# One decoder layer on one core: a 64-byte constant, small weights laid out by the host, and a tail by halves

## The chip, the cores and the metric

The kernel runs on one core of a Trainium2 chip. The metric is device microseconds per execution, the median of several runs. The profile shows one more execution, instruction by instruction.

## The reference

One layer of a hybrid decoder on 512 positions of width 1024, in float32:

```python
def reference(x, ...):
    h = rmsnorm(x, norm_mix_g)
    # h @ w_in, cut into conv gate/value, q, k, v, z of 8 gated-DeltaNet heads, a, b and two merge gates
    # a short gated convolution branch and a gated delta rule branch (chunks of 64), each with an output product
    # sigmoid-gated merge, product with w_o, residual add
    # rmsnorm, conv_ffn: (silu(conv(h @ w_up)[gate]) * conv(...)[value]) @ w_down, residual add
    # final rmsnorm with norm_final_g
...
def rmsnorm(x, g):
    xf = x.astype(jnp.float32)
    y = xf * lax.rsqrt(jnp.mean(xf * xf, axis=-1, keepdims=True) + EPS)
    return (y * g.astype(jnp.float32)).astype(x.dtype)
```

The large products are 1024 to 9216 (and 16 more columns, called ab below), 1024 to 1024 three times, 1024 to 2 x 2816 and 2816 to 1024. The three convolutions have 3 or 4 taps per channel; their weights, the norms' scales and two vectors of 8 numbers per head are the "small weights".

## The kernel before, in words

**Products.** Each float32 operand is split into a rounded part and a rest, which the code calls hi and lo: `wh` and `wl` for weights, `hT[0]` and `hT[1]` for the normalised input, and so on. A product is then three products: hi by lo, lo by hi, hi by hi. Weights come in blocks: one load of 1 MB fills a tile `raw`; `Block.split` makes four pairs wh, wl of it, ACT casting (line 140) and DVE subtracting (line 141), while the block before is used. Nearly all products go through the helper `mm` on line 108, so they differ in a profile by the tiles, where the streaming operand is named first and the stationary one second. In the helper, too, work of other engines is stepped along, after every so many columns. Several products are done in forms that need fewer multiplications: the first with sums of its input (`ts`; for w_up `us`), the product with w_o (`mix`, `mixb`), and the one with w_down (`xs`).

**Where tiles stand.** A tile has the same bytes in all 128 partitions, and each is rounded up to 32 bytes. Pools are stacked from two sides. On the left come the constants (`const`: gate, ident, nhalf, phalf, wA, wF), then the weights (raw, wh, wl), then hT, h, yb and others; on the right what one stage needs (`ts`, `yas`, `mix`, `mixb`, `us`, `xs`). The constants end at byte 2816 of a partition, a multiple of 256, and the sizes that follow are such that every left tile of the products begins at a multiple of 256. The right tiles named here begin at 224 in 256.

**The head** (lines 426 to 575). SP issues the loads in the order of the source. The rows of x are four tiles of 128 rows; the first two are done first: the sum of squares on ACT (`norm_x`), a root on POOL, scaling on DVE (`scale_x`), transposes on PE (`turn_x`), and from PSUM the two parts of hT, `out_hi` on ACT and `out_lo` on DVE. The block K of w_in is loaded in quarters (`load_k`), cast by `round_k` and subtracted by `rest_k`. PE does six products with a tile of zeros (`warm`; three in the program, each runs as two instructions) while it waits. DVE, ACT and POOL follow the source's order here (`manual_schedule`); PE's order is a scheduler's. The small weights arrive as rows (wr, wr2, wr3), are transposed on PE and copied by DVE into wA (scales and conv weights of the first stage) and wF (those of the feed-forward part); dtb and alg are loaded as broadcasts. A scheduler orders what comes behind this block, among it the casts of the next `raw`.

**The tail.** The product with w_down ends with blocks of `LAST` slots: `use_t` twice, then `use_l`. In `use_l` each of the row tiles 2 and 3 takes its last 12 products of 512 columns into one bank of PSUM (`v4`), and `fin2` follows: x-add on DVE, squares on ACT, product with the scale on DVE, the root on POOL, scaling by it of one half on DVE and of the other on ACT, two stores. (The other half of these rows is done earlier, by `fin2_hi`.)

Of the kernel before, what the change touches and what calls it, by code (L numbers as in the profile page):

```python
# [9 lines left out]
F32 = mybir.dt.float32  # L10
# [6 lines left out]
P = 128  # L17
# [42 lines left out]
@with_exitstack  # L60
def layer_kernel(ctx, tc, x, norm_mix_g, w_in, w_ab, conv_a_w, gdn_conv_w, gdn_A_log, gdn_dt_bias,
                 gdn_norm_g, w_a_out, w_b_out, w_o, norm_ffn_g, w_up, ffn_conv_w, w_down,
                 norm_final_g, out):
# [154 lines left out]

    gate = const.tile([1, 1], F32, name="gate")

    def feed(raw):
        el = raw[0:1, 1].rearrange("p k n -> p (k n)") if len(raw.shape) == 4 else raw[0:1, 1]
        tc.keep_in_program_order(pool.tensor_copy(out=gate, in_=el[:, 0:1]))  # L223
        advance(adds, FEED)
# [202 lines left out]
    with tc.tile_pool(name="st1", bufs=1) as st1:  # L427
# [19 lines left out]
        nc.sync.dma_start(out=wr[96:120], in_=conv_a_w.rearrange("o j (c p) -> (o j c) p", p=P))  # L447
        nc.sync.dma_start(out=wr[120:128], in_=norm_mix_g.rearrange("o (c p) -> (o c) p", p=P))
# [7 lines left out]
        load_k(2)  # L456
        dtb = gs.tile([P, H], F32, name="dtb")
        nc.sync.dma_start(out=dtb, in_=gdn_dt_bias[0].partition_broadcast(P))
        alg = gs.tile([P, H], F32, name="alg")
        nc.sync.dma_start(out=alg, in_=gdn_A_log[0].partition_broadcast(P))  # L460
        fr = ffn_conv_w.rearrange("o j (c p) -> (o j c) p", p=P)
        wr2 = st1.tile([66, P], F32, name="wr2")
        nc.sync.dma_start(out=wr2, in_=fr[0:66])
        wr3 = st1.tile([67, P], F32, name="wr3")
        nc.sync.dma_start(out=wr3[0:66], in_=fr[66:132])
        nc.sync.dma_start(out=wr3[66:67], in_=gdn_norm_g)

        po = bank()
        for _ in range(WARM):
            pe.matmul(po[:, 0:512], lhsT=warm[:, 0:P], rhs=warm[:, 0:512], start=True, stop=True)  # L470
        po = bank()
        sst = st1.tile([P, 2 * NT], F32, name="sst")
# [55 lines left out]
        with tc.manual_schedule(engines={mybir.EngineType.DVE, mybir.EngineType.Activation, mybir.EngineType.Pool}):  # L528
# [12 lines left out]
            o_ab, o_k = bank(), [bank(), bank()]  # L541
            for ks in (lower, upper):
                for k in ks:
                    out_hi(0, bs, k)
                for k in ks:
                    out_lo(0, bs, k)
                    k_tile(0, k)
                    ab_tile(k)
                if ks is lower:
                    rest_k(1)  # L550
# [21 lines left out]
        po = bank()  # L572
        pe.transpose(out=po[:, 0:66], in_=wr2, identity=ident[:66, :66])
        pe.transpose(out=po[:, 66:133], in_=wr3, identity=ident[:67, :67])
        dve.tensor_copy(out=wF, in_=po[:, 0:133])

# [655 lines left out]

    def times(o, xs, slot, i, tau, wh, wl, start=False, stop=False, free=False):
        xh, xl = (e[:, slot, i, tau * P:(tau + 1) * P] for e in xs)
        for k, (a, b) in enumerate(((xl, wh), (xh, wl), (xh, wh))):
            mm(o, a, b, start and k == 0, stop and k == 2, free)

# [4 lines left out]

    def times_b(banks, xs, slot, names, tau, wh, wl, q=None, start=False, stop=False):
        for name, i in names:
            o, w = banks["11" if name == "21" else name][tau], name if q is None else (name, q)
            times(o, xs, slot, i, tau, wh[w], wl[w], start and name != "21", stop, name == "21")

# [247 lines left out]
    def use_b(p):  # L1495
        def use(wh, wl):
            if p % 2 == 0 and p // 2 + 1 < N7 // 2:
                splits.append(prep_d(prep_b, p // 2 + 1))
            for name in (*FORMS_T, *FORMS_B):
                for tau in range(2):  # L1500
                    times_b(d_banks, xs(), p % 4, (name,), tau, wh, wl)
            if p == N7 - LAST - 1:
                splits.append(prep_d(prep_b, N7 // 2 - 1))
        return use


    def use_t(q):
        def use(wh, wl):
            for tau in range(2):
                for i in range(2):  # L1510
# [3 lines left out]
        return use  # L1514

    def use_l(wh, wl):
        for tau in range(2):
            for i in range(LAST):
                times_b(d_banks, xs(), (N7 - LAST + i) % 4, FORMS_B, tau, wh, wl, i, False, i == LAST - 1)
            fin2(tau + 2, [d_banks["v4"][tau]])  # L1520

# [14 lines left out]
    def fin2(t, acc):  # L1536
        cvp, x1 = st["cvp"], st["x1"]
        ss = cvp.tile([P, 2], F32, tag="ss", name=nm("ss"))
        if t < 2:
            o = pair_out()  # L1540
            y, r = [o[:, sl] for sl in HALVES], cvp.tile([P, 1], F32, tag="r", name=nm("r"))
        else:
            y, r = st["y", t], st["r", t]
        for hf, a in enumerate(acc):
            sl = HALVES[hf]
            dve.tensor_tensor(out=x1[:, t, sl], in0=x1[:, t, sl], in1=a, op=ALU.add)
            act.activation(out=a, in_=x1[:, t, sl], func=AF.Square, accum_out=ss[:, hf:hf + 1])
            dve.tensor_tensor(out=y[hf], in0=x1[:, t, sl], in1=st["gfn"][:, sl], op=ALU.mult)
            if hf < len(acc) - 1:
                dve.tensor_scalar(r, ss[:, hf:hf + 1], 1.0 / D, EPS, op0=ALU.mult, op1=ALU.add)  # L1550
        dve.scalar_tensor_tensor(out=r, in0=ss[:, len(acc) - 1:len(acc)], scalar=1.0 / D, in1=r,
                                 op0=ALU.mult, op1=ALU.add)
        pool.tensor_tensor(out=r, in0=r, in1=nhalf[:, 0:1], op=ALU.pow)
        dve.tensor_scalar(y[0], y[0], r, None, op0=ALU.mult)
        act.activation(out=y[1], in_=y[1], func=AF.Copy, scale=r)
        for sl, e in zip(HALVES, y):
            nc.sync.dma_start(out=out2[t * P:(t + 1) * P, sl], in_=e)


    def down_place(i):  # L1560
# [18 lines left out]

_INS = ['x', 'norm_mix_g', 'w_in', 'w_ab', 'conv_a_w', 'gdn_conv_w', 'gdn_A_log', 'gdn_dt_bias', 'gdn_norm_g',  # L1580
        'w_a_out', 'w_b_out', 'w_o', 'norm_ffn_g', 'w_up', 'ffn_conv_w', 'w_down', 'norm_final_g']
_OUTS = [((1, 512, 1024), 'float32')]


def laid_out(inputs):

    import numpy as np
# [11 lines left out]
    a["w_in"] = cols(np.concatenate([w[:, :7168], w[:, 7184:]], axis=1))  # L1599
    a["w_ab"] = np.ascontiguousarray(w[:, 7168:7184].reshape(ND, P, 16).transpose(1, 0, 2))  # L1600
    for n in ("w_a_out", "w_b_out", "w_up"):
# [28 lines left out]
```

## Time and profile before

| | |
|---|---|
| runs | 971.88, 973.0, 972.78 us; median 972.78 |
| the profiled execution | 973.09 us, of which the span from the first to the last instruction is 971.4 |
| mean clock granted to TensorE | 0.996 of full speed |
| PE, DVE, ACT, POOL busy | 958.7, 744.0, 506.7, 153.4 us |
| products and transposes on PE | 6166 instructions |
| first product with weights, last product's end | 11.11 us, 963.84 us |
| DMA | 138.11 MB, mean 142 GB/s |

A line of a profile's group reads: code line, engine, operation, output from inputs (buffer numbers left out), partitions x elements, count, then busy microseconds, mean nanoseconds of one, and the engine's idle time just before. A line of waits reads: who waited for whom, then microseconds in total, times, longest. A line of the timeline begins with start and duration in microseconds. A line of windows reads: stretch, its length, busy time and count for each engine, clock, DMA share, GB/s.

### The profile page before, as it was taken

What the parts mean: (1) busy time and instruction counts of PE and PEld (TensorE: products, weight loads), DVE (VectorE), ACT (ScalarE), POOL (GpSimd) and SP (SyncE); (2) the same over time, 40 slices, a digit from 0 to 9 for tenths busy, and PEclk for the clock granted to TensorE, in tenths of its full rate; (3) what the DMA queues carried; (4) which work ended last, traced back from release to release, by engine and by line L of the source; (5) the groups of instructions that cost most, each with busy time, mean ns of one, the idle gap of its engine ahead of it and who ended that gap; (6) DMA issues with size and microseconds to landing.
All of it is one profiled execution on the core that took longest, in us unless ns stands there. A gap on an engine that the chain in (4) does not pass through costs nothing.

```text
span 971.4 us, 16140 instructions
## 1 busy us (share of the span) xinstructions
PE 958.7 (99%) x6166; PEld 826.1 (85%) x6166; DVE 744.0 (77%) x1397; ACT 506.7 (52%) x1071; POOL 153.4 (16%) x251
## 2 busy tenths in 40 slices
PE   8999999999999999999999999999999999999996
PEld 6888887887878889999988888998889998888885
DVE  5968686896725968799853479999978888968775
ACT  6796656565444434344642245555545456546463
POOL 3330300202000212312232100231222210000000
PEclk9999999999999999999999999999999999999999
DMA  6443312213121546756877435594775674075332
GB/s 225 154 138 98 116 53 88 74 58 91 52 88 49 147 121 152 184 151 158 266 222 158 119 120 207 165 244 155 164 185 177 180 154 137 37 282 204 99 130 87
DMA packets 51629, 138.11 MB, mean 142 GB/s; under 512 B 21691, under 2 KB 22112, under 8 KB 42848
## 3 DMA queue, kind: packets, MB, share of 16 engines
q1 hardware_dynamic: 39008, 107.72, 32.3%
q0 software_dynamic: 12544, 29.37, 16.1%
q8 instruction: 48, 0.79, 0.3%
q14 instruction: 29, 0.24, 0.1%
HBM read 133.64 MB, written 32.78 MB: 171 GB/s over the span
## 4 chain that ended last, share of the span: by engine, by line
PE 91%; DVE 3%; ACT 1%; issue 1%; POOL 1%; POOLq 0%
PE ps L108 83%; PE ps L681 1%; PE ps L716 1%; DVE wl L141 1%; PE ps L890 1%; PE ps L910 1%; DVE h L1326 0%; PE ps L899 0%; DVE hn L1312 0%; PE ps L878 0%; PE ps L877 0%; PE ps L854 0%; PE ps L848 0%; POOL r L1310 0%; PE ps L792 0%
## 5 line engine op out<-in xcount | busy, mean ns | idle before, releaser
L108 PE MATMUL ps<-hT,wh 128*128 128x512 f32 (+1 forms) x1104 | 319.3, 369 | 1.6 <-ACT hT L499 1.4
L140 ACT CAST wh<-raw 128x512 fp32r<-128x512 f32 x350 | 203.5, 618 | 212.6 <-PE ps L108 149.1
L141 DVE TENSOR_TENSOR wl<-raw,wh 128x512 fp32r<-128x512 f32 x350 | 233.0, 690 | 58.9 <-ACT wh L140 57.7
L108 PEld LDWEIGHTS ps<-hT,wh 128*128 128x128 f32 x1104 | 197.5, 190 | 30.6 <-ACT hT L499 1.6
L108 PE MATMUL ps<-hT,wl 128*128 128x512 f32 (+1 forms) x552 | 195.5, 362 | 0.0
L108 PE MATMUL ps<-h,wh 128*128 128x512 f32 (+1 forms) x704 | 177.8, 341 | 0.2 <-DVE h L1326 0.2
L108 PEld LDWEIGHTS ps<-h,wh 128*128 128x128 f32 x704 | 122.3, 189 | 15.4 <-DVE h L1326 0.4
L108 PEld LDWEIGHTS ps<-hT,wl 128*128 128x128 f32 x552 | 104.7, 190 | 13.8
L108 PE MATMUL ps<-h,wl 128*128 128x512 f32 (+1 forms) x352 | 114.6, 341 | 0.0
L108 PE MATMUL ps<-wh,xs 128*128 128x512 f32 x312 | 98.2, 395 | 0.0
L108 PEld LDWEIGHTS ps<-h,wl 128*128 128x128 f32 x352 | 66.6, 189 | 7.6
L108 PEld LDWEIGHTS ps<-wh,xs 128*128 128x128 f32 x312 | 58.5, 187 | 14.3
L108 PE MATMUL ps<-wl,xs 128*128 128x512 f32 x156 | 61.6, 395 | 0.0
L223 POOL COPY gate<-raw 1x1 f32<-1x1 f32 x38 | 16.9, 446 | 279.9 <-DMA raw<-in_w_in_dram 119.3
L108 PE MATMUL ps<-ts,wh 128*128 128x256 f32 x320 | 58.5, 281 | 0.0
L338 DVE SCALAR_TENSOR_TENSOR cv<-ps,wA,cv 128x511 f32<-128x511 f32 (+2 forms) x72 | 53.2, 742 | 4.0 <-ACT cv L335 3.8
L140 ACT CAST wh<-raws 128x512 fp32r<-128x512 f32 x66 | 39.2, 619 | 28.2 <-PE ps L108 16.6
L141 DVE TENSOR_TENSOR wl<-raws,wh 128x512 fp32r<-128x512 f32 x66 | 43.1, 689 | 13.4 <-ACT wh L140 13.3
L161 DVE TENSOR_TENSOR raw<-raw 128x512 f32<-128x512 f32 x72 | 49.5, 688 | 1.4
L108 PEld LDWEIGHTS ps<-ts,wh 128*128 128x128 f32 x320 | 49.8, 188 | 0.0
L108 PE MATMUL ps<-us,wh 128*128 128x256 f32 x256 | 46.8, 281 | 0.0
L108 PE MATMUL ps<-yas,wh 128*128 128x512 f32 x128 | 40.4, 395 | 0.0
(310 smaller groups left out, 1548.5 us busy)
## 6 DMA issues: line engine op xcount, KB each, us to landing
raw<-in_w_in_dram SPq DMA_DIRECT2D x35, 1024.0 KB, 4.8
raw<-in_w_up_dram SPq DMA_DIRECT2D x22, 1024.0 KB, 5.7
dv<-in_w_down_dram POOLq DMA_DIRECT2D x50, 256.0 KB, 6.0
raws<-dv SPq DMA_DIRECT2D x8, 768.0 KB, 6.8
ov<-in_w_o_dram POOLq DMA_DIRECT2D x20, 256.0 KB, 5.3
raws<-in_w_down_dram SPq DMA_DIRECT2D x10, 512.0 KB, 4.1
raw<-in_w_a_out_dram SPq DMA_DIRECT2D x4, 1024.0 KB, 5.2
raw<-in_w_b_out_dram SPq DMA_DIRECT2D x4, 1024.0 KB, 5.7
```

What stands on the lines that cost most here:

```text
L108: pe.matmul(o, lhsT=a, rhs=b, start=start, stop=stop, skip_group_check=free)
L140: act.copy(out=wh, in_=src)
L141: dve.tensor_tensor(out=wl, in0=src, in1=wh.bitcast(F32), op=ALU.subtract)
L161: dve.tensor_tensor(out=r[q], in0=a, in1=b, op=op)
L223: tc.keep_in_program_order(pool.tensor_copy(out=gate, in_=el[:, 0:1]))
L338: dve.scalar_tensor_tensor(out=dst[:, sh:], in0=src[:, :S - sh], scalar=wcol(j), in1=dst[:, sh:], op0=ALU.mult, op1=ALU.add)
L681: pe.transpose(out=o[:, n * P:(n + 1) * P], in_=src[:, n * P:(n + 1) * P], identity=ident)
L716: pe.matmul(o[:, i], lhsT=kqs[:, a, h, 0, sl], rhs=kqs[:, b, h, :, sl], start=a > 0, stop=a + b == 0)
L890: pe.matmul(o[:, 0:P], lhsT=TTf[:, f, :], rhs=rs[h], start=True, stop=True)
L910: pe.matmul(o[:, 0:P], lhsT=A[:, f, :], rhs=vns[h], start=True, stop=True)
```

## The change

**Addresses.** `gate`, of which one element is used, becomes 64 bytes instead of 4 (which take 32), and wF becomes part of a tile `rest_w` of 596 bytes (608 with rounding, 544 before) that also holds dtb and alg. The constants end at byte 2912 instead of 2816: every left tile moves by 96 bytes and now begins at 96 in 256. The right tiles stay where they were.

**Head.** The host lays out the small weights, in three loads: `small_mix` straight into wA, `small_ab`, and `small_rest` into rest_w. The transposes of wr, wr2, wr3 and the copies from PSUM are gone. K's first quarter is the fifth load, wA the sixth. PE is put under the order of the source as well, with a few more products of zeros (`busy`) in the waits for x; `first_tiles` orders the first products per k. `rest_k(0)` and `rest_k(1)` now come behind the second `out_lo` of each half.

**Tail.** `use_l` is written out anew, in source order on DVE, ACT, POOL and SP. Tile 3's last 12 products become 24 of 256 columns, first all of the low half, then all of the high half in a bank of its own, and what follows is done by halves. The last store goes out from ACT's queue. For the second bank, `use_t` adds what v4 holds of the high half into x1 ahead (one more add of 128x256 on DVE).

```diff
-    gate = const.tile([1, 1], F32, name="gate")
+    gate = const.tile([1, 16], F32, name="gate")
...
-    wF = const.tile([P, 133], F32, name="wF")
+    rest_w = const.tile([P, 133 + 2 * H], F32, name="rest_w")
+    wF = rest_w[:, 0:133]
+    dtb, alg = rest_w[:, 133:133 + H], rest_w[:, 133 + H:133 + 2 * H]
...
         load_x(0)
         load_x(1)
-        wr = st1.tile([P, P], F32, name="wr")
-        nc.sync.dma_start(out=wr[0:96], in_=gdn_conv_w.rearrange("o j (c p) -> (o j c) p", p=P))
...
+        load_k(0)
+        nc.sync.dma_start(out=wA, in_=small_mix)
         ab_raw = st1.tile([P, ND, 16], F32, name="ab_raw")
-        nc.sync.dma_start(out=ab_raw, in_=w_ab)
-        load_k(0)
+        nc.sync.dma_start(out=ab_raw, in_=small_ab)
         load_k(1)
...
+        nc.sync.dma_start(out=rest_w, in_=small_rest)
...
+        def first_tiles(ks, q):
+            for i, k in enumerate(ks):
+                out_lo(0, bs, k)
+                if i == 1:
+                    rest_k(q)
+                for e in (0, 1):
+                    mm(o_k[0][:, 0:HS], piece(k_block.wh, 0, k), hT[e][:, k, 0:HS], k == 0 and e == 0, False)
+                ab_tile(k)
+            for k in ks:
+                mm(o_k[0][:, 0:HS], piece(k_block.wl, 0, k), hT[0][:, k, 0:HS], False, k == ND - 1)
...
             norm_x(0)
             scale_x(0)
             turn_x(0, bs)
-            pe.transpose(out=po[:, 0:P], in_=wr, identity=ident)
+            busy(3, P)
             norm_x(1)
             round_k(0)
-            dve.tensor_copy(out=wA, in_=po[:, 0:P])
             scale_x(1)
             turn_x(1, bs)
+            busy(2, P)
             ab_split()
             round_k(1)
-            rest_k(0)
...
+    def use_l(wh, wl):
+        def part(t, e, a, cols, between):
...
+            for i in range(LAST):
+                times_b(d_banks, xs(), (N7 - LAST + i) % 4, FORMS_B, t - 2, wh, wl, i, e == 1 and i == 0, i == LAST - 1,
+                        cols, a)
+            dve.tensor_tensor(out=x1[:, t, cols], in0=x1[:, t, cols], in1=a[:, cols], op=ALU.add)
+            act.activation(out=a[:, cols], in_=x1[:, t, cols], func=AF.Square, accum_out=ss[:, e:e + 1])
+            between()
+            dve.scalar_tensor_tensor(out=r, in0=ss[:, e:e + 1], scalar=1.0 / D, in1=r, op0=ALU.mult, op1=ALU.add)
...
+            part(2, 0, d_banks["v4"][0], slice(0, S), lambda: mult(2, slice(0, S)))
+            power(2)
+            part(3, 0, d_banks["v4"][1], LO, between)
+            part(3, 1, d_banks["r"][0], HI, lambda: mult(3, HI))
+            power(3)
+            scale(2, 1, False, nc.sync)
+            scale(3, 0, False, nc.sync)
+            scale(3, 1, True, nc.scalar)
```

On ACT, in the second half of the head (the x rows of tiles 2 and 3; L509 and L503 are the casts of K's last quarters, L499 and L493 `out_hi`, L140 and L139 the casts of the next block), before:

```order
L480 ACTIVATE sq_274,sst<-xt_134 128x1024
L509 CAST wh_278<-raw_102 128x512
L499 ACTIVATE hT_81<-ps_315,wA 128x256 x2
L499 ACTIVATE hT_81<-ps_316,wA 128x256 x2
L499 ACTIVATE hT_81<-ps_317,wA 128x256 x2
L499 ACTIVATE hT_81<-ps_318,wA 128x256 x2
L140 CAST wh_406<-raw_394 128x512
L140 CAST wh_418<-raw_394 128x512
L140 CAST wh_432<-raw_394 128x512
L140 CAST wh_463<-raw_394 128x512
```

and now:

```order
L474 ACTIVATE sq_265,sst<-xt_131 128x1024
L503 CAST wh_269<-raw_102 128x512
L139 CAST wh_393<-raw_381 128x512
L139 CAST wh_405<-raw_381 128x512
L139 CAST wh_419<-raw_381 128x512
L139 CAST wh_450<-raw_381 128x512
L493 ACTIVATE hT_81<-ps_306,wA 128x256 x2
L493 ACTIVATE hT_81<-ps_307,wA 128x256 x2
L493 ACTIVATE hT_81<-ps_308,wA 128x256 x2
L493 ACTIVATE hT_81<-ps_309,wA 128x256 x2
```

The four casts of the next block have moved ahead of the eight `out_hi`; on DVE the four subtractions have moved ahead of the eight `out_lo` in the same way.

On DVE, in the first half of the head (L513 and L507 are `rest_k`, L503 and L497 `out_lo`), before:

```order
L392 TENSOR_TENSOR ab_114<-ab_raw,ab_114 128x8x16
L513 TENSOR_TENSOR wl_201<-raw_102,wh_183 128x512
L503 SCALAR_TENSOR_TENSOR hT_82<-ps_153,wA,hT_81 128x256 x2
L503 SCALAR_TENSOR_TENSOR hT_82<-ps_154,wA,hT_81 128x256 x2
L513 TENSOR_TENSOR wl_234<-raw_102,wh_199 128x512
L503 SCALAR_TENSOR_TENSOR hT_82<-ps_155,wA,hT_81 128x256 x2
```

and now:

```order
L394 TENSOR_TENSOR ab_114<-ab_raw,ab_114 128x8x16
L497 SCALAR_TENSOR_TENSOR hT_82<-ps_141,wA,hT_81 128x256 x2
L507 TENSOR_TENSOR wl_205<-raw_102,wh_173 128x512
L497 SCALAR_TENSOR_TENSOR hT_82<-ps_142,wA,hT_81 128x256 x2
L497 SCALAR_TENSOR_TENSOR hT_82<-ps_143,wA,hT_81 128x256 x2
L507 TENSOR_TENSOR wl_235<-raw_102,wh_190 128x512
```

The first subtraction of K stands behind the first pair of `out_lo` instead of ahead of it, the second behind the third pair instead of the second.

On DVE, the last rows of the program (o is the tile before, y those of tiles 2 and 3), before:

```order
L1546 TENSOR_TENSOR x_6414<-x_6414,ps_9763 128x512
L1554 TENSOR_SCALAR o_10162<-o_10162,r_10163 128x512
L1548 TENSOR_TENSOR y_9842<-x_6414,gfn 128x512
L1551 SCALAR_TENSOR_TENSOR r_9844<-ss_10189,r_9844 128x1
L1554 TENSOR_SCALAR y_9842<-y_9842,r_9844 128x512
L1546 TENSOR_TENSOR x_6414<-x_6414,ps_9764 128x512
L1548 TENSOR_TENSOR y_9866<-x_6414,gfn 128x512
L1551 SCALAR_TENSOR_TENSOR r_9868<-ss_10211,r_9868 128x1
L1554 TENSOR_SCALAR y_9866<-y_9866,r_9868 128x512
```

and now:

```order
L1547 SCALAR_TENSOR_TENSOR r_9831<-ss_10167,r_9831 128x1
L1544 TENSOR_TENSOR x_6401<-x_6401,ps_9751 128x256
L1525 TENSOR_TENSOR y_9853<-x_6401,gfn 128x256
L1547 SCALAR_TENSOR_TENSOR r_9855<-ss_10185,r_9855 128x1
L1544 TENSOR_TENSOR x_6401<-x_6401,ps_9752 128x256
L1525 TENSOR_TENSOR y_9853<-x_6401,gfn 128x256
L1547 SCALAR_TENSOR_TENSOR r_9855<-ss_10204,r_9855 128x1
L1532 TENSOR_SCALAR y_9830<-y_9830,r_9831 128x512
L1532 TENSOR_SCALAR y_9853<-y_9853,r_9855 128x512
```

Tile 2's scaling (y_9842 before, y_9830 now), which needs POOL's root, has moved from ahead of tile 3's add to behind everything of tile 3 but its own scaling.

More of the change, by code (lines that the diff above doesn't have):

```diff
@@ L456, in layer_kernel, with busy @@
         load_k(2)
[L457 to L466, printed above, removed]
+        nc.sync.dma_start(out=rest_w, in_=small_rest)
         po = bank()
-        for _ in range(WARM):
-            pe.matmul(po[:, 0:512], lhsT=warm[:, 0:P], rhs=warm[:, 0:512], start=True, stop=True)
-        po = bank()
+        def busy(n, cols):
+            for _ in range(n):
+                pe.matmul(po[:, 0:cols], lhsT=warm[:, 0:P], rhs=warm[:, 0:cols], start=True, stop=True)
+        busy(WARM, S)
         sst = st1.tile([P, 2 * NT], F32, name="sst")
@@ L527, in layer_kernel @@
         k_block.ready = True
-        with tc.manual_schedule(engines={mybir.EngineType.DVE, mybir.EngineType.Activation, mybir.EngineType.Pool}):
+        with tc.manual_schedule(engines={mybir.EngineType.DVE, mybir.EngineType.Activation, mybir.EngineType.Pool,
+                                         mybir.EngineType.PE}):
             norm_x(0)
@@ L571, in layer_kernel @@
                     out_lo(HS, bs, k)
[L572 to L575, printed above, removed]
     gdn_w = lambda c: (lambda j: wA[:, j * 24 + c:j * 24 + c + 1])
@@ L1500, in use @@
                 for tau in range(2):
[L1501 removed]
+                    times_b(d_banks, xs(), p % 4, (name,), tau, wh, wl, None, False,
+                            p == N7 - LAST - 1 and name in FORMS_B)
             if p == N7 - LAST - 1:
@@ L1504, in use_b @@
         return use
+    LO, HI = slice(0, HS), slice(HS, S)
     def use_t(q):
         def use(wh, wl):
+            if q == 1:
+                x1 = st["x1"]
+                dve.tensor_tensor(out=x1[:, 3, HI], in0=x1[:, 3, HI], in1=d_banks["v4"][1][:, HI], op=ALU.add)
             for tau in range(2):
@@ L1516, in use_l, with mult, scale, power @@
     def use_l(wh, wl):
-        for tau in range(2):
-            for i in range(LAST):
-                times_b(d_banks, xs(), (N7 - LAST + i) % 4, FORMS_B, tau, wh, wl, i, False, i == LAST - 1)
-            fin2(tau + 2, [d_banks["v4"][tau]])
+        x1, gfn = st["x1"], st["gfn"]
+        def mult(t, cols):
+            dve.tensor_tensor(out=st["y", t][0][:, cols], in0=x1[:, t, cols], in1=gfn[:, cols], op=ALU.mult)
+        def scale(t, hf, on_act, queue):
+            y, r = st["y", t][hf], st["r", t]
+            if on_act:
+                act.activation(out=y, in_=y, func=AF.Copy, scale=r)
+            else:
+                dve.tensor_scalar(y, y, r, None, op0=ALU.mult)
+            queue.dma_start(out=out2[t * P:(t + 1) * P, HALVES[hf]], in_=y)
+        def power(t):
+            pool.tensor_tensor(out=st["r", t], in0=st["r", t], in1=nhalf[:, 0:1], op=ALU.pow)
+        def part(t, e, a, cols, between):
+            r = st["r", t]
+            ss = st["cvp"].tile([P, 2], F32, tag="ss", name=nm("ss"))
+            for i in range(LAST):
+                times_b(d_banks, xs(), (N7 - LAST + i) % 4, FORMS_B, t - 2, wh, wl, i, e == 1 and i == 0, i == LAST - 1,
[4 more added lines that the diff above has]
+            dve.scalar_tensor_tensor(out=r, in0=ss[:, e:e + 1], scalar=1.0 / D, in1=r, op0=ALU.mult, op1=ALU.add)
+        def between():
+            mult(3, LO)
+            scale(2, 0, True, nc.sync)
+        with tc.manual_schedule(engines={mybir.EngineType.DVE, mybir.EngineType.Activation, mybir.EngineType.Pool,
+                                         mybir.EngineType.SP}):
+            part(2, 0, d_banks["v4"][0], slice(0, S), lambda: mult(2, slice(0, S)))
[6 more added lines that the diff above has]
+            scale(3, 1, True, nc.scalar)
     def fin2_hi(t):
```

67 lines of the change are left out of this document (29 added, 38 removed).

## The prediction

> **What bounds the kernel now.** I read the line of busy times first, then what TensorE (PE) waited for, its groups of products by form, and the timeline of both ends.
>
> ```profile
> PE 958.7 (99%) x6166; PEld 826.1 (85%) x6166; DVE 744.0 (77%) x1397; ACT 506.7 (52%) x1071; POOL 153.4 (16%) x251
> ...
> PE ps L470 <- DVE warm L431: 1.5, 1, 1.5
> PE ps L108 <- ACT hT L499: 1.4, 1, 1.4
> PE ps L496 <- DVE xr L491: 1.1, 1, 1.1
> PE ps L681 <- DVE vs L929: 0.5, 1, 0.5
> ```
>
> PE is busy for 958.7 of the span's 971.4 us, and its waits are few: the three longest, 4.0 us in all, are of the head (warm, xr, hT), the next is half a microsecond. So three things can move the time: what PE's products cost, when the stream of products gets going, and what follows the last product. The change touches all three.
>
> **Part 1: the addresses.** The products dominate, so I start there. By the tiles' sizes, everything on the left side (weights wh and wl, hT, h, yb) begins at a multiple of 64 bytes in a partition before, and 32 bytes beyond one now; what lies on the right (yas, ts, us, xs, mix, mixb) is 32 bytes beyond one in both. The groups by form split along this line:
>
> ```profile
> L108 PE MATMUL ps<-h,wh 128*128 128x512 f32 x384 | 119.8, 389 | 0.0
> L108 PE MATMUL ps<-wh,xs 128*128 128x512 f32 x312 | 98.2, 395 | 0.0
> L108 PE MATMUL ps<-wl,xs 128*128 128x512 f32 x156 | 61.6, 395 | 0.0
> ...
> L108 PE MATMUL ps<-h,wh 128*128 128x256 f32 x320 | 60.8, 284 | 0.2 <-DVE h L1326 0.2
> ...
> L108 PE MATMUL ps<-ts,wh 128*128 128x256 f32 x320 | 58.5, 281 | 0.0
> L108 PE MATMUL ps<-us,wh 128*128 128x256 f32 x256 | 46.8, 281 | 0.0
> L108 PE MATMUL ps<-yas,wh 128*128 128x512 f32 x128 | 40.4, 395 | 0.0
> ...
> L108 PE MATMUL ps<-yb,wh 128*128 128x512 f32 x128 | 39.6, 389 | 0.0
> ...
> L108 PE MATMUL ps<-wh,mix 128*128 128x512 f32 x88 | 28.2, 396 | 0.0
> ```
>
> Column "mean ns of one": at 512 columns, products of two left tiles take 389, those with one right tile 395 to 398. These are lengths of pipelined instructions; what counts is the pitch from one start to the next. The cleanest place is where 192 products with yas end and 192 with yb begin, with the same kind of weights:
>
> ```profile
> 489.38 0.40 PE L108 MATMUL ps<-yas,wh 128*128 128x512 f32 x1
> ...
> 534.19 0.39 PE L108 MATMUL ps<-yb,wh 128*128 128x512 f32 x1
> ...
> 577.74 0.39 PE L108 MATMUL ps<-wh,mix 128*128 128x512 f32 x1
> ```
>
> (534.19 - 489.38)/192 = 233.4 ns against (577.74 - 534.19)/192 = 226.8 ns: 6.6 ns apart, at full clock in both. It isn't the DMA traffic: two stretches of the down stage, all products with xs, hold equally many at twice the traffic (the DMA share is the last number but one).
>
> ```profile
> 870.00:910.00 40.00, 40.00 (x173) 1.00 0.57 193
> 915.00:955.00 40.00, 40.00 (x173) 1.00 0.26 86
> ```
>
> What no row shows is two operands that are both 32 bytes off. I bound it from both sides. If the cost comes from the two operands standing differently (relative), all 512-column products with a right tile fall to 226.8 and nothing rises: xs 312 + 156, yas 128 + 64, mix 88 + 44, mixb 24 + 12, so 828 x 6.6 = -5.5 us (counts from the same view by form, of which the largest groups stand above). If it comes from any operand off the 64 bytes (absolute), those stay and the 1968 left-left ones (hT 1200, h 576, yb 192) rise: +13.0 us. At 256 columns the sign is the other way, 281 for ts and us against 284 for h; I take 2 ns a product: relative, 480 + 384 = 864 products lose 1.7 us; absolute, the 936 left-left ones gain 1.9. I take relative, -5.5 + 1.7 = -3.8 us, because of one more thing in the rows, where the streaming operand is named first and the stationary one second: the tile that is off streams in one group (yas past wh) and is the stationary one in another (wh past xs), and the price is the same 395; a penalty of one tile's own address should differ between the operand that is loaded once and the one that streams. For ACT, DVE and the loads I found no row that splits by address and cost the shift at nothing; were there a cost, PE's stream covers it, as DVE is busy for 77% of the span and ACT for 52%.
>
> The Trainium skill, page "TensorE: Matmul & The Clock Gate", section "Step-by-step: what each phase is for", says that the two operands of a product come through two independent read ports and that loading the next weights takes nothing from the running product. By that rule an address has no price, this term is 0 and rival a below holds; the trace shows 6.6 ns between two streams that differ in the place of one operand, so here the row decides against it.
>
> **Part 2: the head.** The removed pieces (the transposes of wr, wr2, wr3, DVE's copies of wA and wF, five of 18 loads) stand where PE or DVE had room or are short: wF's transposes and copy went between other waits of the chain below. What sets the end of the head is a chain, ACT's casts, then ACT's hT, DVE's hT, DVE's scaling of the third and fourth row tile, their transposes, and hT again:
>
> ```profile
> 11.90:15.30 3.40, 3.31 (x16) 3.06 (x16) 3.40 (x11) 3.40 (x9) 0.00 (x0) 0.53 0.90 259
> ```
>
> (a window, its PE clock is the 0.53) and from the timeline:
>
> ```profile
> 10.40 0.69 DVE L513 TENSOR_TENSOR wl<-raw,wh 128x512 fp32r<-128x512 f32 x1
> 10.59 2.66 ACT L499 ACTIVATE hT<-ps,wA 128x256 fp32r<-128x256 f32 x7
> ...
> 11.45 1.66 DVE L503 SCALAR_TENSOR_TENSOR hT<-ps,wA,hT 128x256 fp32r<-128x256 f32 x4 [0.36 <-ACT hT L499]
> ...
> 13.07 5.10 SPq L135 DMA_DIRECT2D raw<-in_w_in_dram  x2
> ...
> 18.24 0.75 DVE L491 TENSOR_SCALAR xr<-xt,rt 128x1024 f32<-128x1024 f32 x1 [0.44 <-POOL rt L486]
> ...
> 19.42 1.91 PE L496 MATMUL ps<-ident,xr 128*128 128x128 f32 x16
> 20.71 3.03 ACT L499 ACTIVATE hT<-ps,wA 128x256 fp32r<-128x256 f32 x8 [3.99 <-PE ps L496]
> 21.58 3.23 DVE L503 SCALAR_TENSOR_TENSOR hT<-ps,wA,hT 128x256 fp32r<-128x256 f32 x8 [2.59 <-ACT hT L499]
> ...
> 23.58 2.22 ACT L140 CAST wh<-raw 128x512 fp32r<-128x512 f32 x4
> ...
> 24.93 1.89 DVE L141 TENSOR_TENSOR wl<-raw,wh 128x512 fp32r<-128x512 f32 x3
> ...
> 26.87 0.43 PE L609 MATMUL ps<-ident,abT 32*128 32x32 f32 x4
> ```
>
> K's first quarter as the fifth load starts ACT's casts sooner, but the second quarter, behind as many bytes as before, still has to be cast ahead of hT: the 10.59 becomes 10.1 to 10.6, I take 10.3. DVE's first subtraction (10.40, then in a gap of DVE) now stands behind the first pair of hT, so 0.69 us enter its chain: 11.45 + 3.83 = 15.28 becomes 11.15 + 4.5 = 15.65, and the last scaling ends at about 19.4 instead of 18.99. Before, the transposes stood behind PE's own backlog until 19.42 and the last of them gave ACT its start at 20.71; PE now gets there with less behind it (the stream ran at 0.53 of its clock in that window, half of which the fillers may save), so they end at about 20.4 and ACT starts at about 19.9, 0.8 sooner. Against that, four casts (2.2 us) and four subtractions of 0.69 for the next block now stand ahead of ACT's and DVE's second hT. DVE does them from 19.4 to 22.2, and its eight hT (3.23) end at 25.4 instead of 24.81; but the same four subtractions are gone from behind, and PE's wait is shorter at both ends, so abT's transposes come at about 26.4 instead of 26.87. Term: -0.5 us. The ends: -1.5 if DVE's hT are ready for PE when it asks (the whole 0.8, plus the fillers and the earlier start), +0.8 if the casts wait for their weights (the loads that began to be issued at 13.07 and took until 18.17), and all of the 0.69 and more passes through. PE's order puts the hi-by-lo products one behind the other per k, so that it waits for DVE's hT at 0.41 us each; that is cover for PE, not extra work.
>
> **Part 3: the tail.**
>
> ```profile
> 963.45 0.39 PE L108 MATMUL ps<-wh,xs 128*128 128x512 f32 x1
> 963.64 0.16 DVE L1551 SCALAR_TENSOR_TENSOR r<-ss,r 128x1 f32<-128x1 f32 x1 [0.28 <-ACT ps L1547]
> ...
> 964.45 0.49 DVE L1554 TENSOR_SCALAR y<-y,r 128x512 f32<-128x512 f32 x1 [0.65 <-POOL r L1553]
> 964.85 0.68 DVE L1546 TENSOR_TENSOR x<-x,ps 128x512 f32<-128x512 f32 x1
> ...
> 965.62 0.60 ACT L1547 ACTIVATE ps<-x 128x512 f32<-128x512 f32 x1 [0.46 <-DVE x L1546]
> ...
> 966.62 0.54 POOL L1553 TENSOR_TENSOR r<-r,nhalf 128x1 f32<-128x1 f32 x1 [2.21 <-DVE r L1551]
> 967.20 0.72 ACT L1555 ACTIVATE y<-y,r 128x512 f32<-128x512 f32 x1 [0.85 <-POOL r L1553]
> ```
>
> The last product ends at 963.84, but DVE's last add begins at 964.85, since a scaling of the tile before, waiting for POOL, stands ahead of it. Now the first half is added right after 963.80, at half the length of the 0.68 (0.35, an estimate), multiplied (0.35), its squares summed meanwhile; then the second half: add ends 965.3, squares 965.85, root on POOL to 966.7. The last scalings begin at about 966.75 instead of 967.20, and the two last stores go out on two queues rather than one behind the other: -0.45 to -0.85. Against it, 24 products of 256 columns in place of 12 of 512 (24 x 120 - 12 x 233 = +0.07), and one more add of 128x256 on DVE, in the stage where DVE had waited 4.79 us for PE, so covered:
>
> ```profile
> 954.78 1.39 DVE L1546 TENSOR_TENSOR x<-x,ps 128x512 f32<-128x512 f32 x2 [4.79 <-PE ps L108]
> ```
>
> Term: -0.5, ends -1.2 and +0.2.
>
> **Sum.** Address -3.8, head -0.5, tail -0.5: -4.8 us. The profiled execution took 973.09 (span 971.4 and 1.7 around it), 0.3 above the median 972.78 of the runs; the sum is a difference, so I take it from the median: 968.0 us.
>
> **The rivals.** (a) Addresses make no difference when both are moved, or the price hangs on a distance that the shift doesn't close (left and right tiles then stand 128 bytes apart in 256, where left and left stand 0 apart): 972.78 - 1.0 = 971.8, too little to tell from no change, which here means within 0.2%, or 1.9 us. For it: the rows show one distance only. (b) Slower: the penalty is absolute. Then the 1968 left-left products rise: +13.0 - 1.9 - 1.0 = 982.9. For it: right tiles, the only ones off 64 bytes, are the only slow ones. Against: the same 395 in both roles. It decides from 1.0 us / 1968 = 0.5 ns for each of these products on. (c) The head gives back: raw lands late, ACT's casts hold its hT, DVE's subtractions hold its own, +0.8, with no gain from addresses and -0.2 of the tail: 973.4, no change to measure.
>
> **Chances.** Forecast 0.60 (its own range 965 to 970.5), (a) 0.22, (b) 0.12, (c) 0.06. The range 965.0 to 972.8 holds the forecast and (a), 0.82. Faster by over 0.2% (below 970.8): the forecast and a little of (a) with a good head, 0.64. Within: the rest of (a) and (c), 0.22. Slower: (b) and a bit for what I haven't seen, 0.14.
>
> **What would show it.** Right: the groups xs, yas, mix and mixb fall from 395 or more to about 389, h, hT and yb stay, and PE's busy time falls by about 4 us. Wrong in part 1: yb and h rise to 395 (absolute), or nothing moves. Head: abT's transposes at about 26.4; if they come after 27, the casts and subtractions put ahead are the cause. Tail: from the last product's end to the end of the span 7.0 instead of 7.56 us.

## The result: 7 us slower, and where the time went

The changed kernel took 978.89 us (median of 5 runs, 977.86 to 979.34) where the kernel before took 971.88 (5 runs, 970.99 to 973.0): ratio 1.0068, interval 1.0055 to 1.0082. The forecast was 968.0, in a range of 965.0 to 972.8; the time lies outside it, on the other side.

The profiled execution of the changed kernel took 977.86 with a span of 976.0, 4.8 more than the profiled one before (973.09 and 971.4). The one is the fastest of its kernel's runs and the other slower than any of its own, so the pair shows less than the medians. The same two views as before, busy times and what PE waited for:

```profile
PE 960.5 (98%) x6185; PEld 828.7 (85%) x6185; DVE 743.9 (76%) x1399; ACT 505.0 (52%) x1071; POOL 156.2 (16%) x251
...
PE ps L107 <- DVE kn L699: 2.9, 1, 2.9
PE ps L654 <- DVE G L644: 1.6, 1, 1.6
PE ps L463 <- DVE warm L433: 1.5, 1, 1.5
PE ps L490 <- DVE xr L485: 1.1, 2, 0.6
PE ps L107 <- DVE hT L497: 0.7, 2, 0.5
```

Two waits are new and stand on top: for kn and for G, both of the delta rule's preparation, at 45 to 62 us, where PE waited for nothing before. To see what else moved, I matched PE's products of the two traces one by one and took the difference of their starts. The changed kernel is 1.1 us ahead from 30 to 45 us, 0.7 behind from 48 to 58, 5.4 behind at 74, and then runs beside the other for 890 us: 5.5 behind at 490 and at 575, 5.7 at 850, 5.3 at the last product. At the end of the span it is 4.6 behind. So the stage from 45 to 74 us lost 6.5 us, the tail won 0.7, and the whole of the products in between, the part that I had priced at -3.8, moved by less than half a microsecond.

Where the 6.5 us lie is read from the starts of the same products in both timelines. Between 45 and 48 us, at the wait for G, PE goes from 1.1 ahead to 0.7 behind: 1.8 us. The rest, before:

```profile
57.42 1.03 PE L681 MATMUL ps<-ident,kq 128*128 128x128 f32 x8
58.21 0.48 PE L108 MATMUL ps<-hT,wh 128*128 128x512 f32 x1
...
61.97 2.20 PE L108 MATMUL ps<-hT,wh 128*128 128x512 f32 x9
```

and in the changed kernel:

```profile
58.09 1.03 PE L678 MATMUL ps<-ident,kq 128*128 128x128 f32 x8
62.06 0.50 PE L107 MATMUL ps<-hT,wh 128*128 128x512 f32 x1 [2.94 <-DVE kn L699]
...
67.44 2.22 PE L107 MATMUL ps<-hT,wh 128*128 128x512 f32 x9
```

From the eight transposes to the first product behind them it takes 3.97 us instead of 0.79, the wait for kn; the sixteen products from there to the last line take 5.38 instead of 3.76. Why these are slow is seen in PE's windows of the changed kernel (columns as before, PE alone):

```profile
59.13:62.06 2.93, 0.00 (x0) 1.00 0.00 0
62.06:62.79 0.73, 0.73 (x3) 0.98 0.00 0
62.79:66.20 3.41, 3.41 (x10) 0.50 0.02 5
66.20:70.19 3.99, 3.99 (x18) 1.00 0.21 33
```

After 2.93 us with nothing to do, and 0.73 us after it has gone on, PE's clock falls to a half for 3.41 us: the seven products that lie wholly in it take about 430 ns each instead of 230. So 1.8 for G, 3.2 for kn and 1.6 for the half clock, which is the 6.5 within a tenth.

The Trainium skill, page "TensorE: Matmul & The Clock Gate", section "HAM oscillation — how this bites in real kernels", warns of idle gaps of PE over about 3.4 us, after which the clock is halved. The trace agrees on the half clock, and shows it after a gap of 2.93 us.

The 1.1 us that PE is ahead from 30 to 45 us are not won by the new head. The profiled execution before ran 3.4 us of its head at half clock (the prediction's window 11.90:15.30, at 0.53), the changed kernel's did not; nor did that of "the right side in step" below, which has the old head. In that window, PE alone, it and then the changed kernel show:

```profile
11.90:15.30 3.40, 3.40 (x31) 1.00 0.83 252
...
11.90:15.30 3.40, 3.21 (x27) 1.00 0.82 339
```

So these two can be compared. ACT's first hT and the transposes of abT, old head, then new:

```profile
10.16 3.02 ACT L499 ACTIVATE hT<-ps,wA 128x256 fp32r<-128x256 f32 x8
25.23 0.43 PE L609 MATMUL ps<-ident,abT 32*128 32x32 f32 x4
...
9.83 3.02 ACT L493 ACTIVATE hT<-ps,wA 128x256 fp32r<-128x256 f32 x8
26.02 0.43 PE L606 MATMUL ps<-ident,abT 32*128 32x32 f32 x4
```

From the one to the other it is 15.07 us with the old head and 16.19 with the new one. The other profiles of this study with a head at full clock agree: 15.07 to 15.10 in three more of the old head, 16.17 to 16.22 in four more of the new one (the last experiment, which splits the first eight hT, left out); the profile before, with its half clock, has 16.28. At equal clock the new head loses 1.1 us there. Nor do the waits at 45 to 62 us come from a PE that is early: in the profile of "the right side in step" it transposes G at 44.65 and waits for nothing from 40 to 80 us; in the changed kernel it comes to the same place at 45.70, later, and waits.

The wait for kn comes from the order of ACT's work. kn needs the sums of squares (`junk`) of eight pieces; before, all eight come first, and the table load, vT and the exponentials of Dm follow. ACT's timeline before:

```profile
55.63 0.28 ACT L701 ACTIVATE junk<-ps 128x128 f32<-128x128 f32 x1
55.80 0.19 ACT L701 ACTIVATION_READ_ACCUMULATOR junk<-ps 128x1 f32 x1
56.01 1.28 ACT L965 ACT_TABLE_LOAD   x1
57.31 0.63 ACT L965 ACTIVATE vT<-cv 128x512 f32<-128x512 f32 x1
```

And in the changed kernel, the same engine and place (line numbers are 3 lower), with DVE's kn:

```profile
55.23 0.28 ACT L698 ACTIVATE junk<-ps 128x128 f32<-128x128 f32 x1
55.40 0.19 ACT L698 ACTIVATION_READ_ACCUMULATOR junk<-ps 128x1 f32 x1
...
56.38 2.46 ACT L595 ACTIVATE Dm<-Dm,negG 128x128 f32<-128x128 f32 x8 [0.79 <-POOL Dm L587]
58.73 0.26 ACT L698 ACTIVATE junk<-ps 128x128 f32<-128x128 f32 x1
...
59.10 1.28 ACT L962 ACT_TABLE_LOAD   x1
60.40 0.63 ACT L962 ACTIVATE vT<-cv 128x512 f32<-128x512 f32 x1
60.94 0.26 ACT L698 ACTIVATE junk<-ps 128x128 f32<-128x128 f32 x1
...
61.32 0.69 DVE L699 TENSOR_TENSOR kn<-ps,kdv 128x512 f32<-128x512 f32 x1 [4.33 <-ACT junk L698]
```

ACT waits 0.79 us for POOL's Dm, does eight exponentials, one sum, a table load, vT, and only then the last sum. DVE has waited 4.33 us for it, PE 2.9 for DVE. G is the same kind of case on DVE:

```profile
45.84 0.68 DVE L140 TENSOR_TENSOR wl<-raw,wh 128x512 fp32r<-128x512 f32 x1
46.44 0.74 DVE L337 SCALAR_TENSOR_TENSOR cv<-ps,wA,cv 128x510 f32<-128x510 f32 x1
47.10 0.18 DVE L644 COPY G<-ps 128x32 f32<-128x32 f32 x1
```

The copy of G, begun at 45.97 before, stands behind one more subtraction and a later convolution step; PE waits 1.6 us for it.

None of these lines is in the diff. The scheduler orders all work behind the head's fixed block, and with a different head it came to a different order, which the order of the instructions shows before any run. ACT, before (left of the bar) and now:

```
ssk (5th to 8th sum)  x4                | ssk (5th, 6th)
ACT_TABLE_LOAD, vT                      | Dm exponentials  x8
ACT_TABLE_LOAD                          | ssk (7th)
Dm exponentials  x8                     | ACT_TABLE_LOAD, vT
                                        | ssk (8th)
```

The groups by form show that the addresses did next to nothing to the 6 ns:

```profile
L107 PE MATMUL ps<-wh,xs 128*128 128x512 f32 x304 | 95.4, 395 | 0.0
...
L107 PE MATMUL ps<-yas,wh 128*128 128x512 f32 x128 | 40.6, 396 | 0.0
...
L107 PE MATMUL ps<-yb,wh 128*128 128x512 f32 x128 | 39.6, 389 | 0.0
```

xs and yas stay at 395 and 396, yb at 389: neither my forecast nor the absolute rival (b), but what rival (a) says of a distance that the shift doesn't close.

### The profile page after: what moved, and what is told of

It is laid out like the page before. It is cut to its first block, busy times and chain, and to the rows that moved or that the text cites. A ratio compares the mean times of both kernels' runs of the same rounds, so it can differ in the third digit from the quotient of the medians.

```text
span 976.0 us, 16173 instructions
## 1 busy us (share of the span) xinstructions
PE 960.5 (98%) x6185; PEld 828.7 (85%) x6185; DVE 743.9 (76%) x1399; ACT 505.0 (52%) x1071; POOL 156.2 (16%) x251
## 4 chain that ended last, share of the span: by engine, by line
PE 87%; DVE 6%; ACT 2%; DMA 2%; issue 2%; POOL 1%; SPq 0%; POOLq 0%; DVEq 0%; ACTq 0%
PE ps L107 80%; DVE wl L140 2%; PE ps L678 1%; DMA raw<-in_w_in_dram 1%; PE ps L713 1%; DVE cv L337 1%; PE ps L887 1%; PE ps L907 1%; DVE hT L497 1%; DVE hn L1310 1%; ACT Dm L595 1%; DVE h L1324 0%; PE ps L896 0%; PE ps L875 0%; PE ps L874 0%
## 5 line engine op out<-in xcount | busy, mean ns | idle before, releaser
L139 ACT CAST wh<-raw 128x512 fp32r<-128x512 f32 x350 | 203.7, 617 | 224.4 <-PE ps L107 155.8
L140 DVE TENSOR_TENSOR wl<-raw,wh 128x512 fp32r<-128x512 f32 x350 | 233.0, 690 | 62.7 <-ACT wh L139 61.7
L107 PE MATMUL ps<-wh,xs 128*128 128x512 f32 (+1 forms) x320 | 98.3, 389 | 0.0
L107 PE MATMUL ps<-wl,xs 128*128 128x512 f32 (+1 forms) x160 | 62.3, 389 | 0.0
L139 ACT CAST wh<-raws 128x512 fp32r<-128x512 f32 x66 | 39.3, 618 | 27.8 <-PE ps L107 16.1
L140 DVE TENSOR_TENSOR wl<-raws,wh 128x512 fp32r<-128x512 f32 x66 | 43.0, 686 | 13.2 <-ACT wh L139 13.1
```

The costliest lines, as they stand in the source:

```text
L107: pe.matmul(o, lhsT=a, rhs=b, start=start, stop=stop, skip_group_check=free)
L139: act.copy(out=wh, in_=src)
L140: dve.tensor_tensor(out=wl, in0=src, in1=wh.bitcast(F32), op=ALU.subtract)
```

## The experiments

Each was timed in runs that alternate with the kernel before; times are medians.

**The shift alone** (e1_shift). The kernel before, all engines in its own order, with left tiles 96 bytes on:

```diff
-    gate = const.tile([1, 1], F32, name="gate")
+    gate = const.tile([1, 16], F32, name="gate")
...
+    dtb = const.tile([P, H], F32, name="dtb")
+    alg = const.tile([P, H], F32, name="alg")
```

> The kernel before with its left tiles moved by 96 bytes alone (gate of 64 bytes, and dtb and alg as constants of their own); the order of every engine is that of before. Theory A (the order of ACT's and DVE's work at 45 to 62 us costs the time, addresses nothing): within 1 us of before, the products with yas, xs and mix at the same pitch of 232 to 234 ns and those of two left tiles at 227. Rival B (the shift itself costs a part of the 7 us that the runs show but the one profile shows only as 4.8): 1.5 to 2.5 us slower.

972.68 us against 972.2 before, ratio 1.0 (0.9991 to 1.0009). The shift is worth nothing, as theory A has it. The pitches, taken from start to start, are 232.4 for xs, 233.3 for yas and 226.8 for yb.

**The tail alone** (e2_tail), on the kernel before.

> The kernel before with the new tail alone. Theory A: 0.8 us faster than before (the lag of PE's stream in the changed kernel falls by 0.8 in the last 10 us), with PE's stream up to 955 us unchanged. Rival B (the tail's gain is lost, since the halves cost as much on DVE as they save): 0 to 0.2.

971.61 against 972.2, ratio 0.9993 (0.9984 to 1.0001): 0.6 us, and the interval reaches to nothing. In its profile the span ends 7.3 us after the last product, 7.6 before.

**The head alone** (e5_head): the changed kernel with the tail of before.

> The changed kernel with the tail of before: head and shift, no new tail. Theory A (the head brings the new order of ACT's and DVE's work at 45 to 62 us, and with it all of the loss): the waits of PE for G (1.6 us) and kn (2.9 us) and the half clock behind them are there; 979.5, as the changed kernel plus the 0.6 that the tail brought alone. Rival B (the loss needs the tail and the head together, by the scheduler): under 975.

978.58, ratio 1.0065 (1.0051 to 1.0079). The head, with the shift, holds the whole loss; its profile has the same two waits:

```profile
PE ps L107 <- DVE kn L699: 3.0, 1, 3.0
PE ps L654 <- DVE G L644: 1.7, 1, 1.7
```

**The copies of G first** (e3_root_first). The changed kernel, one edit:

```diff
-        dve.tensor_copy(out=G, in_=o3[:, 0:32])
-        dve.tensor_copy(out=Gl, in_=o3[:, 32:64])
+        with tc.high_priority():
+            dve.tensor_copy(out=G, in_=o3[:, 0:32])
+            dve.tensor_copy(out=Gl, in_=o3[:, 32:64])
```

> The changed kernel with one thing altered: DVE's two copies of G and Gl get a higher priority in the scheduler, by which they move ahead of a convolution step and the eight exponentials of Dm on ACT move behind the last sum of squares that kn needs. Theory A: the waits of PE for kn (2.9 us) and the 3 us at half clock behind it go (-4.8 us), of the wait for G (1.6 us) about 0.6 goes: 5 to 5.5 us faster than the changed kernel, so at 973.5. Rival B (the weights' load ahead of gtd on SP's queue is what holds the chain): under 1 us faster, the wait moves to Dm.

973.46, 5.4 less than the changed kernel, ratio to before 1.0014 (1.0004 to 1.0023). kn is gone from PE's waits, G is left with 1.2. The loads' order on SP's queue is that of the changed kernel, so rival B falls.

**The exponentials last** (e9_exps), which separates the two waits. The call that emits them moves behind the sums of squares; G stays late:

```diff
-        if pr == 0:
-            exps(0)
-        Dm = Dms.pop(pr)
...
+        if pr == 0:
+            exps(0)
+        Dm = Dms.pop(pr)
         dve.tensor_scalar(sk, ssk, EPS, None, op0=ALU.add)
```

> The changed kernel with the eight exponentials of Dm traced behind the last sum of squares instead of ahead of the first; DVE's copies of G stay where the change put them. Theory A (two separate prices: 1.6 us for G, and 2.9 of waiting for kn plus 1.9 of half clock behind it for the exponentials that stand ahead of the sums of squares on ACT): PE's wait for kn goes, that for G stays at 1.6; 4.5 to 5 us faster than the changed kernel, at 974.0. Rival (the chain of G holds both, and kn would wait anyway): 977 or more.

973.5, ratio to before 1.0018 (1.0009 to 1.0026): 5.4 us from eight instructions of ACT that stand behind the sums of squares again. PE's waits are then led by

```profile
PE ps L654 <- DVE G L644: 1.6, 1, 1.6
```

So the price of kn and of the half clock behind it is shown by itself, half a microsecond above my estimate. The scheduler shifted other work of ACT and DVE along with the eight; G's 1.6 is all that PE waits for from 40 to 80 us.

**The transpose of G later** (e6_later), on top of "the copies of G first": two more `yield` ahead of it.

> The kernel of the run e3_root_first (the changed kernel with the copies of G first) with the transpose of G traced two slabs of products later, so that PE reaches it when DVE has copied G. Theory A (what is left of the loss against before is PE's wait for G, 1.2 us): that wait is gone, 1.0 to 1.5 us faster than e3_root_first, at 972.2. Rival B (the chain of G, gtd and Dm gets longer by the delay and kn or U waits for it): as e3_root_first or slower, 973.5 to 975.

972.42, ratio 0.9997 (0.9988 to 1.0006). G is gone from PE's waits, and the time is that of before. In this run's profile PE waits 1.8 us for the first hT instead, which the last experiment takes up.

**The right side in step** (e4_right). The kernel before, with 224 bytes above the right side's tiles:

```diff
+        p3.enter_context(tc.tile_pool(name="pr3", bufs=1, side="right")).tile([P, 56], F32, name="pr3")
         sc = st["sc"] = p3.enter_context(tc.tile_pool(name="sc", bufs=1, side="right"))
...
+        ctx.enter_context(tc.tile_pool(name="pr4", bufs=1, side="right")).tile([P, 56], F32, name="pr4")
         up = st["up"] = ctx.enter_context(tc.tile_pool(name="up", bufs=1, side="right"))
```

> The kernel before with 224 bytes of padding above the right side's tiles, so that they begin at a multiple of 256 bytes like the left ones; no instruction is moved. Theory C (the pitch hangs on the two operands' distance in 256 bytes, which the change took from 224 to 128 and not to 0): 828 products of 512 columns fall from 233 to 227 ns, 864 of 256 columns rise by up to 2 ns: 3.5 to 5.5 us faster than before, at 966.5 to 968.5. Rival D (it hangs on the region of the memory, or on the tile, and not on the low bits of the address): no change, 971.9, the pitch of yas stays at 233.

968.63 against 972.2, ratio 0.9962 (0.9949 to 0.9974), with no instruction moved. All groups of 512 columns come to one price, those of 256 columns rise from 281 to 283:

```profile
L108 PE MATMUL ps<-wh,xs 128*128 128x512 f32 x312 | 96.3, 389 | 0.0
...
L108 PE MATMUL ps<-ts,wh 128*128 128x256 f32 x320 | 59.2, 283 | 0.0
L108 PE MATMUL ps<-us,wh 128*128 128x256 f32 x256 | 47.4, 283 | 0.0
...
L108 PE MATMUL ps<-yas,wh 128*128 128x512 f32 x128 | 39.6, 389 | 0.0
L108 PE MATMUL ps<-yb,wh 128*128 128x512 f32 x128 | 39.6, 389 | 0.0
```

The time lies 0.1 beyond the forecast's upper end, and rival D falls: the low bits of the address count, and where the change brought the tiles, 128 apart in 256, isn't like enough. That it is the distance of the two operands, as theory C has it, and not the place 224 of one of them, is not shown at 512 columns: in every slow group one operand stood at 224, and no run had both there. From start to start xs now takes 226.7 ns and yas 226.7.

**Tail and right side together** (e7_tail_right).

> The kernel before with the new tail and the right side's tiles at a multiple of 256 bytes. If the two are independent, 968.63 - 0.6 = 968.0; if the tail's gain hung on something that the padding changes, 968.6 or more.

968.24, ratio 0.9959 (0.9946 to 0.9971): as the sum.

**Like at 512 columns, unlike at 256** (e8_skew). ts and us are slices that begin 224 bytes into a tile of 256 bytes more.

> As e7_tail_right, but ts and us, which are used in products of 256 columns alone, begin 224 bytes beyond a multiple of 256 as they did before; yas, xs, mix and mixb stay at the multiple. Theory C (at 256 columns the like distance costs 1.7 ns a product, 120.0 against 118.3, as the traces of before and of e4_right show): 864 x 1.7 = 1.5 us faster than e7_tail_right, at 966.5. Rival: the difference at 256 columns is that of the neighbours in the stream (after a product of h or hT), and nothing is won: 968.0.

967.0, ratio 0.9948 (0.9935 to 0.996), 1.2 below the run before. The runs of the two overlap; what settles it is the pitch of ts and us, 118.3 ns again where it was 120.0. The two groups return to 281 while xs stays at 389:

```profile
L108 PE MATMUL ps<-wh,xs 128*128 128x512 f32 x304 | 93.8, 389 | 0.0
...
L108 PE MATMUL ps<-ts,wh 128*128 128x256 f32 x320 | 58.5, 281 | 0.0
L108 PE MATMUL ps<-us,wh 128*128 128x256 f32 x256 | 46.8, 281 | 0.0
```

**All together** (e10_all): the changed kernel, G repaired, the right side in step with the left, ts and us out of step.

> The kernel of e6_later (head, tail, G first, its transpose later) with the right side's tiles at the left side's place in 256 bytes (96) and ts and us 224 beyond: e6_later took 972.4, the two placings gave 3.6 and 1.2 us on the kernel before, so 967.6; as e8_skew took 967.0 without the new head, the head then brings nothing. Rival (on this kernel PE waits for DVE or ACT where its products get shorter): 969 or more.

967.31, ratio 0.9948 (0.9935 to 0.9962): no better than without the new head. A part of what the head loses is seen on ACT in this run:

```profile
7.78 0.62 ACT L503 CAST wh<-raw 128x512 fp32r<-128x512 f32 x1 [0.68 <-DMA raw<-in_w_in_dram]
...
10.66 0.62 ACT L503 CAST wh<-raw 128x512 fp32r<-128x512 f32 x1 [2.07 <-DMA raw<-in_w_in_dram]
11.19 3.02 ACT L493 ACTIVATE hT<-ps,wA 128x256 fp32r<-128x256 f32 x8
```

K's first quarter is cast 1.6 us sooner than before (9.34), but hT waits for the second, whose load lands at another time in each run: ACT waited for it 2.07 us here, 0.39 in the changed kernel's profile, 1.25 in e5_head, 1.66 in e3_root_first, 2.32 in e9_exps and 2.63 in e6_later.

**K's second quarter cast later** (e11_k1_late), behind the first four hT, on the kernel of "all together":

```diff
             ab_split()
-            round_k(1)
...
             for q, ks in enumerate((lower, upper)):
+                if q:
+                    round_k(1)
                 for k in ks:
                     out_hi(0, bs, k)
```

> As e10_all, with one cast moved: K's second quarter is cast behind the first four hT of ACT instead of ahead of them. In the changed kernel ACT waited 0.4 us for that quarter's load before any hT, in three other runs of the same head 1.3 to 2.6 us, while K's first quarter, now the fifth load, had been cast 1 us earlier. If that wait holds the head: 0.7 to 1.5 us faster than e10_all, and the runs lie closer together. Rival (what follows, x's third and fourth tile or DVE, holds the end of the head): within 0.3 us.

965.36 (965.14 to 965.9), ratio 0.9931 (0.9919 to 0.9943): 1.9 us below "all together", more than I gave it, and with it the best kernel of this study, 6.6 us or 0.7% faster than before. ACT's first hT, at the same place:

```profile
7.45 0.62 ACT L503 CAST wh<-raw 128x512 fp32r<-128x512 f32 x1 [0.56 <-DMA raw<-in_w_in_dram]
8.02 0.30 ACT L393 CAST ab<-ab_raw 128x128 fp32r<-128x128 f32 x1
9.15 1.57 ACT L493 ACTIVATE hT<-ps,wA 128x256 fp32r<-128x256 f32 x4 [0.83 <-PE ps L490]
10.59 0.64 ACT L503 CAST wh<-raw 128x512 fp32r<-128x512 f32 x1
```

hT now waits for PE's transposes of x and for no load, the five runs lie within 0.8 us, and PE's waits for xr and ACT's hT, 1.2 each in "all together", are gone. hT begins 2.04 us sooner than there and the transposes of abT, at 25.38, 1.98 sooner, so the 1.9 us are the head's. With this the new head is as early as the old one at full clock (25.11 to 25.25 in three profiles, 26.27 in one where hT began only at 11.20), and no earlier. Why this kernel is still 1.6 us below "like at 512 columns, unlike at 256" wasn't taken apart; a wait of PE for G, 0.4 in that one's profile, is gone.

## Why the prediction was wrong

- **The step that failed is the end of part 2.** I summed the head up to abT's transposes, and took it that whatever PE gained there it would keep. But the new head also gave ACT and DVE a new order from 45 to 62 us, and that cost 6.5 us in the profiles, of which taking the exponentials out of the way brought 5.4 back in the runs. I showed the moved rows of the head and did not price those behind it, though PE's busy share of 100% there says that nothing waits and not how much slack there is.
- **The gain of part 2, -0.5, isn't there either, and its sum came near by luck.** The transposes came at 26.02 (forecast 26.4, before 26.87). But the 26.87 belongs to an execution with 3.4 us of half clock in its head, the window that I read as the old head's usual course; of six profiles of the old head two have it. At full clock the new head takes 1.1 us more from hT to abT and not less: 0.6 up to ACT's second eight hT (9.54 us behind the first instead of 8.93), 0.5 behind it. Which of the moved pieces costs how much wasn't taken apart. And hT, for which I took 10.1 to 10.6, began at 9.83 to 11.29, with the wait for K's second quarter. Rival (c) had the sign and about the size of this, +0.8, for reasons that weren't tested, and not the 6.5 behind it.
- **Part 1, the address term, -3.8, came to nothing.** The reason that I gave was right as far as it went, relative and not absolute: yb stayed at 226.8, which ends rival (b). What failed is the bound itself: I let the change's new distance count as none, and wrote the 128 bytes in 256 that remain only into rival (a), which was right on this part. With both sides at the same place in 256 the term is -3.6 us, close to the -3.8.
- **Part 3, the tail**, -0.5: 7.56 us after the last product became 6.86 in the changed kernel's profile (forecast 7.0). But the head alone, with the old tail, has 7.23 and the tail alone 7.30, so the profiles give the new tail 0.3 to 0.4 us, and the runs of the tail alone 0.6 with an interval that holds 0. The step holds within its ends, and its size isn't clear of the noise. (Two slips on which no term turns: 24 x 120 - 12 x 233 is +0.08, and six of 19 loads go, not five of 18.)
- **The range** was built from terms each of which had a place in the diff. The 5 us lay where the diff has no line.
- **What stays open.** The medians differ by 7.0, the two profiles by 4.8. About 1.2 of the 2.2 between is the half clock in the head of the profile before (16.28 us from hT to abT instead of 15.07), which ran 1.2 above its median. The other 1.0 would be covered by the changed head's wait for K's second quarter, the shortest of six in its profile (0.39 against 1.25 to 2.63); it wasn't shown run by run. Nor was it taken apart which edit of the head turned the scheduler's order; the addresses alone and the tail alone leave the order of the other parts as it was.

## What to carry to other kernels

Where a scheduler orders what follows, a change has two diffs: the one in the source and the one in the order, and the second has to be priced along its whole length, above all ACT and DVE around every chain that ends in a wait of PE. A wait of PE of 2.9 us cost 4.8 here, through the clock. Before two profiles are subtracted, their clocks have to be compared window by window: a stretch at half clock in the one alone made a loss of 1.1 us look like a gain. And when products of one shape fall into two prices, line up the places of both operands, not of one: two pads of 224 bytes gave 3.6 us here, where every engine's order stayed the same.

## What the runs showed of the hardware

The pitch of products of 512 columns hangs on where the two operands stand within 256 bytes of a partition: 226.7 to 227 ns at distance 0 (both at 0, or both at 96), 233.3 for xs at 224, 232.4 for xs and 233.3 for yas at 128. At 256 columns it is the other way, 120.0 ns for ts and us at distance 0, 118.7 at 128 and 118.3 at 224; there it goes by the distance and not by one tile's place, as ts at 224 with weights at 0 and ts at 64 with weights at 96 both take 118.3. At 512 columns the two weren't separated, since the slow operand always stood at 224. Other distances weren't tried.

The Trainium skill, page "TensorE: Matmul & The Clock Gate", section "Step-by-step: what each phase is for", has the two operands come through independent ports; the experiment with the right side in step shows that where they stand is nevertheless worth 6 to 7 ns a product.

PE's clock changes in all thirteen profiles lie a multiple of 3.41 us apart. Up to 70 us there are five stretches of 3.41 us at half clock, and in the 3.41 us ahead of each PE was busy for 0.69 to 1.79 us, so never quite idle; in the others of this raster, from the first full clock on, it was busy for 1.76 us or more, with one exception of 1.54. In the head of before, waits of 1.4 us and less were enough for it.
